# Eleven semaphores fewer in a batched a·bᵀ kernel: stores counted on the loads' semaphores and on five shared ones

## The chip, the cores and the metric

One core of a Trainium2 chip. The metric is the device time of one execution in microseconds (us), as the median of several executions. The record marks each execution as slow when it is over 1.5% above the fastest of its kernel. A ratio and its 95% interval are the record's, from the fast runs of the same rounds, so a ratio is not quite that of the medians quoted beside it. A profile is one execution; its span runs from the first instruction to the last and is about 1.8 us shorter than the measured time.

## The reference

```python
def setup_inputs():
    batch, m, k, n = 16, 512, 512, 512
    return {"a": randn(batch, m, k), "b": randn(batch, n, k)}      # float32

def reference(a, b):
    return np.matmul(a, b.transpose(0, 2, 1)).astype(np.float32)
```

Sixteen products of 512 x 512 matrices: 33.55 MB are read, 16.78 MB written.

## The kernel before

Every engine has its own program; semaphores tie them together. SyncE loads pairs of matrices (16 loads of 2 MB) into seven slots and stores outputs 8 to 15. The first load of b goes out on ScalarE's queue. GpSimd stores outputs 0 to 7 and watches landings to hand the seven output buffers back to ScalarE. VectorE casts to bfloat16, TensorE transposes and multiplies, ScalarE copies the products from PSUM (the memory that TensorE writes to) to the output buffers.

A complete transfer has added 16 to its semaphore: the trace has 16 landings for each, one by one. Each load slot has a semaphore, and so has each of the 16 stores. At the end of the program GpSimd sets all semaphores that the program allocated to zero (`EVENT_SEMAPHORE_RANGE_CLEAR` in the profile, called the clearing below); that instruction is not in the source, the framework adds it.

```python
    STORES = "SSSSOSOSOSSOOOOOO"               # GpSimd: S = store, O = wait for the next landing
    LATE = {11: (8, 9), 13: (10, 11), 15: (12, 13)}
    ...
        s_ld = [sem(f"s_ld{i}") for i in range(NL)]        # NL = 7
        s_st = [sem(f"s_st{i}") for i in range(batch)]     # 16
    ...
        def landed(n):
            return s_st[n], 16

        def store(n):
            engine = nc.gpsimd if n < STORES.count("S") else nc.sync
            engine.wait_ge(s_out, n + 1)
            engine.dma_start(out[n]..., ob[:, n % NO]).then_inc(s_st[n], 16)    # NO = 7

        load(0)
        load(1, nc.scalar)
        for n in range(2, NL):
            load(n)
        for n in range(2 * pairs):
            nc.sync.wait_ge(s_ld[n % NL], 16 * (n // NL + 1)).then_inc(s_go, 1)
            if n > 0 and n + NL - 1 < 2 * pairs:
                load(n + NL - 1)
            for m in LATE.get(n, ()):
                store(m)
        store(batch - 2)
        store(batch - 1)
        for n in range(batch - NO, batch - 1):
            nc.sync.wait_ge(*landed(n))

        n_st = n_of = 0
        nc.gpsimd.wait_ge(s_ld[0], 32)
        for what in STORES:
            if what == "S":
                store(n_st); n_st += 1
            else:
                nc.gpsimd.wait_ge(*landed(n_of)).then_inc(s_of, 1); n_of += 1
    ...     # ScalarE takes one s_of (an output buffer that is free) per output
```

## Time and profile before

| | before |
|---|---|
| median time | 125.56 us (3 runs, 125.42 to 125.84) |
| span of the profile | 123.7 us |
| bytes moved | 50.33 MB |
| rate in mid-stream | 419 to 430 GB/s |
| last copy of ScalarE, last issue of a store | 113.7 us |
| last landing | 122.3 us |
| from there to the end of the span | 1.4 us |

The compute engines finish 8.6 us before the last landing. The lines themselves, and what they say of the bound, stand in the prediction.

### The profile page before, as it was taken

The page shows a single profiled execution, that of the slowest core. Times are in us where ns is not written, and L with a number is a line of the kernel's source. Part 1 is how long each engine was busy: PE and PEld are TensorE (multiplying, and loading weights), DVE is VectorE, ACT ScalarE, POOL GpSimd, SP SyncE. Part 2 cuts the span into 40 slices and gives each one's busy share as a digit, 9 for nine tenths or more (in the row PEclk, how much of TensorE's full clock was granted, in tenths as well). Part 3 has the DMA queues.
Part 4 walks back from the last instruction along what each step waited for, and adds up shares of the span by engine and source line. Part 5 has one row for each costly group of instructions (what it writes and reads, how often), then busy time and mean ns, then how long its engine had stood idle before and what let it go on. Part 6 is the DMA issues. An engine that isn't in the chain of part 4 may idle for free. (4 is left out here: it accounts for less than half of the span.)

```text
span 123.7 us, 2364 instructions
## 1 busy us (share of the span) xinstructions
PE 90.8 (73%) x768; PEld 55.9 (45%) x768; DVE 68.1 (55%) x96; ACT 68.0 (55%) x130; POOL 5.2 (4%) x14
## 2 busy tenths in 40 slices
PE   0000189999999899989998999999899919995000
PEld 0000177447644754674476347645754528441000
DVE  0000698983895689289918974865957078400000
ACT  4000065478855956795589369765946069655000
POOL 2000000000000250001010110000000000000000
PEclk9999999999999999999999999999999986999955
DMA  4999999999999999999999999999999999999990
GB/s 148 413 435 429 429 429 424 429 424 435 435 424 424 429 392 363 445 416 424 453 405 437 443 408 443 424 424 458 397 445 427 408 429 427 429 427 429 424 387 8
DMA packets 4608, 50.33 MB, mean 407 GB/s; under 512 B 512, under 2 KB 512, under 8 KB 512
## 3 DMA queue, kind: packets, MB, share of 16 engines
q1 hardware_dynamic: 3312, 39.85, 76.2%
q0 software_dynamic: 1152, 8.39, 16.1%
q10 hardware_dynamic: 144, 2.10, 4.2%
HBM read 33.55 MB, written 16.78 MB: 407 GB/s over the span
## 5 line engine op out<-in xcount | busy, mean ns | idle before, releaser
L249 PE MATMUL ps<-tb,ta 128*128 128x512 bf16 x256 | 57.8, 379 | 0.5
L207 ACT COPY ob<-ps 128x512 f32 x64 | 34.4, 589 | 29.2 <-PE ps L249 21.3
L189 ACT COPY ta<-tp 128x512 bf16<-128x512 bf16 x64 | 32.9, 610 | 15.0 <-PE tp L230 15.0
L249 PEld LDWEIGHTS ps<-tb,ta 128*128 128x128 bf16 x256 | 24.1, 98 | 30.6 <-issue 4.0
L230 PE MATMUL tp<-ident,ha 128*128 128x128 bf16 x256 | 19.3, 228 | 18.1 <-PEq L135 18.1
L230 PEld LDWEIGHTS tp<-ident,ha 128*128 128x128 bf16 x256 | 16.3, 102 | 21.9 <-issue 20.1
L170 DVE COPY tb<-tp 128x1024 bf16<-128x1024 bf16 x32 | 21.2, 684 | 4.2 <-DVEq L135 4.2
L230 PE MATMUL tp<-ident,hb 128*128 128x128 bf16 x256 | 18.5, 230 | 3.4 <-PEq L135 3.4
L230 PEld LDWEIGHTS tp<-ident,hb 128*128 128x128 bf16 x256 | 16.3, 103 | 4.0 <-issue 4.0
L154 DVE CAST ha<-ld 128x1024 bf16 x8 | 5.5, 687 | 14.3 <-DVEq L135 14.3
L165 DVE COPY ha<-wa 128x2048 bf16<-128x2048 bf16 x8 | 5.5, 691 | 12.7 <-DVEq L135 12.7
L160 DVE CAST wa<-ld 128x2048 bf16 x8 | 9.8, 1220 | 0.0
L160 DVE CAST wb<-ld 128x2048 bf16 x8 | 9.7, 1217 | 0.0
L154 DVE CAST hb<-ld 128x1024 bf16 x8 | 5.5, 692 | 7.3 <-DVEq L135 7.3
L103 POOL DMA_DIRECT2D out_dram<-ob x8 | 4.5, 570 | 65.5 <-DMA ld<-in_b_dram 40.9
L169 DVE COPY hb<-wb 128x2048 bf16<-128x2048 bf16 x8 | 5.5, 685 | 0.1
L157 DVE CAST ha<-ld 128x1024 bf16 x8 | 5.5, 686 | 0.0
L157 DVE CAST hb<-ld 128x1024 bf16 x8 | 5.5, 686 | 0.0
L180 ACT ACT_TABLE_LOAD x1 | 1.3, 1283 | 1.5 <-SPq L43 1.5
L79 POOL TENSOR_SCALAR_AFFINE_SELECT ident<-ident 128x128 bf16<-128x128 bf16 x1 | 0.3, 283 | 0.2 <-POOL ident L77 0.2
L77 POOL MEMSET ident<- 128x128 bf16 x1 | 0.2, 204 | 0.5 <-SPq L43 0.5
L180 ACT COPY one<-const-float32-1.0 128x1 f32<-128x1 f32 x1 | 0.2, 192 | 0.0
(4 smaller groups left out, 0.4 us busy)
## 6 DMA issues: line engine op xcount, KB each, us to landing
ld<-in_a_dram SPq DMA_DIRECT2D x8, 2048.0 KB, 26.5
ld<-in_b_dram SPq DMA_DIRECT2D x7, 2048.0 KB, 29.6
out_dram<-ob POOLq DMA_DIRECT2D x8, 1024.0 KB, 28.9
out_dram<-ob SPq DMA_DIRECT2D x8, 1024.0 KB, 19.7
ld<-in_b_dram ACTq DMA_DIRECT2D x1, 2048.0 KB, 12.0
```

Source lines behind the costliest of these rows:

```text
L103: engine.dma_start(out[n].rearrange("(p j) n -> p j n", j=J), ob[:, n % NO]).then_inc(s_st[n], 16)
L154: nc.vector.tensor_copy(out=h[:, :J, :], in_=src[:, :J, :HK]).then_inc(s_cd, 1)
L157: nc.vector.tensor_copy(out=h[:, J:, :], in_=src[:, J:, :HK]).then_inc(s_c, 1)
L160: nc.vector.tensor_copy(out=w[:], in_=src[:, :, HK:]).then_inc(s_w, 1)
L165: nc.vector.tensor_copy(out=ha[:], in_=wa[:]).then_inc(s_ca, 1)
L169: nc.vector.tensor_copy(out=hb[:], in_=wb[:]).then_inc(s_cb, 1)
L170: nc.vector.tensor_copy(out=tb[:, ko, :], in_=tp[:, 2 + ko % 2].rearrange("k j p -> k (j p)"),).then_inc(s_eb, 1)
L180: nc.scalar.copy(out=one[:], in_=nc.const_aps.tensor(1.0, (P, 1), f32))
L189: c = nc.scalar.copy(out=ta[:, ko, e * J * P:(e + 1) * J * P].rearrange("k (j p h) -> k j p h", j=J, h=2), in_=tp[:, ko % 2, :, e * HP:(e ...
L207: c = nc.scalar.copy(out=dst[:, j, :].rearrange("m (p j) -> m p j", j=2 * J), in_=ps[:, j, :].rearrange("m (j p) -> m p j", j=2 * J),)
L230: t = nc.tensor.transpose(tp[:, 2 * x + g, j, :], h[:, j, g * P:(g + 1) * P], ident[:])
L249: t = nc.tensor.matmul(ps[:, j, :], ta[:, ko, (e * J + j) * P:(e * J + j + 1) * P], tb[:, ko, :].rearrange("k (j p) -> k j p", j=2 * J)[:, ...
```

## The change

The intent is to need fewer semaphores: 34 in place of 45 (of those that the program clears at its end). GpSimd's eight stores take turns on five. SyncE's eight stores count on the semaphores of load slots, with a threshold that counts the loads before them. The description of the change also named the first load of b on ScalarE's queue, but the kernel before already has it there.

```diff
+    SW = 5
-        s_st = [sem(f"s_st{i}") for i in range(batch)]
+        s_st = [sem(f"s_st{i}") for i in range(SW)]
         def landed(n):
-            return s_st[n], 16
+            if n < STORES.count("S"):
+                return s_st[n % SW], 16 * (n // SW + 1)
+            slot = (n - STORES.count("S") + 2) % NL
+            return s_ld[slot], 16 * (len(range(slot, 2 * pairs, NL)) + 1 + (n - STORES.count("S") >= NL))
         ...
-            ).then_inc(s_st[n], 16)
+            ).then_inc(landed(n)[0], 16)
```

## The prediction

> **What bounds the kernel now.** I read four views, in this order: the page's table of 40 slices, its part on DMA queues with the table of stretches, the waits of the DMA-issuing queues, and the one source line that holds the end of the program.
>
> The slices first, because they say which resource is full and when:
>
> ```profile
> PE   0000189999999899989998999999899919995000
> DVE  0000698983895689289918974865957078400000
> ACT  4000065478855956795589369765946069655000
> DMA  4999999999999999999999999999999999999990
> ```
>
> Only the DMA row is at 9 from the second slice to the last but one. TensorE, VectorE and ScalarE start four slices late and have dips; they follow the loads. The bytes and the rate:
>
> ```profile
> HBM read 33.55 MB, written 16.78 MB: 407 GB/s over the span
> ```
>
> 33.55 + 16.78 = 50.33 MB have to move, whatever the semaphores are. The table of stretches (start:end, length, busy time of five engines, granted clock, DMA share, GB/s) shows that the rate is flat:
>
> ```profile
> 10.00:30.00 20.00, 14.09 (x123) 9.62 (x124) 13.47 (x19) 8.97 (x18) 0.00 (x0) 1.00 1.01 430
> 60.00:90.00 30.00, 28.31 (x262) 17.75 (x261) 21.29 (x31) 22.16 (x45) 1.68 (x3) 1.00 1.01 428
> 114.00:118.00 4.00, 0.00 (x0) 0.00 (x0) 0.00 (x0) 0.00 (x0) 0.00 (x0) 1.00 1.01 428
> 120.00:121.00 1.00, 0.00 (x0) 0.00 (x0) 0.00 (x0) 0.00 (x0) 0.00 (x0) 0.50 0.30 123
> ```
>
> 50.33 MB at 428 GB/s are 117.6 us. The span is 123.7 us; the other 6.1 us lie at the two ends: about 1.5 us before data flow and a ramp after it (the first 4 us moved 197 GB/s, which is 4.0 x (1 - 197/428) = 2.2 us lost), and from about 120.3 us on the tail, 3.4 us. The compute is over by 114 us: the last 4 us of full-rate transfers run with no engine busy. The kernel is a full-rate stream of transfers with a start and an end that nothing covers. The chain of waits on the page accounts for only 9% PE and 1% ACT, because it ends at the last ScalarE copy before the last store; the transfers behind that store aren't in it, so here it isn't the view to go by.
>
> The end, from the waits of SyncE's queue (waited for, us in total, times, longest) and from the line that closes the program (durations in ns min/median/max, then start in us):
>
> ```profile
> SPq L121 <- DMA out_dram<-ob: 5.7, 3, 2.4
> SPq L289 <- DMA out_dram<-ob: 1.7, 1, 1.7
> L289 SPq EVENT_SEMAPHORE  x5: 17/28/1680, 120.5 to 123.6; - x5
> L289 POOLq DRAIN  x3: 34/129/714, 120.1 to 123.4; - x3
> L289 POOLq EVENT_SEMAPHORE_RANGE_CLEAR  x1: 287/287/287, 123.1 to 123.1; - x1
> ```
>
> SyncE waits 1.7 us for the last store (the 1680 ns instruction), which lands at about 122.3 us. Then follow a barrier, one instruction of GpSimd that sets the program's semaphores to zero (287 ns at 123.1 us), and another barrier. This last part, 1.4 us, is the only place of the profile where the number of semaphores can show.
>
> **What the Trainium skill says.** "DMA: Bandwidth & Descriptors", section "Why a DMA increments its semaphore by 16 and not by 1", says that each of the 16 transfer engines adds 1 after its own data, and that two transfers in flight on one semaphore can satisfy a wait too early. So sharing is only safe if the first has been waited for before the second is issued; otherwise it costs a race or an added wait. The trace shows the order that the sharing needs, below. The same page, "Anatomy of one DMA — SWDGE (gpsimd) path", gives about 100 ns for the semaphore update after the receipt of the last write, and calls the write of the semaphore on trn2 nearly free: the cost is per transfer, not per semaphore. The number of transfers doesn't change (32 in all). The kernel before agrees in what can be seen: 4-byte packets take 9 ns against 309 ns for an 8192-byte one in the records of the transfers. Its table under "Specifications" names 435 GB/s as the ceiling of the fabric; the steady 428 GB/s here are 98% of it, and the 358 GB/s that it gives as HBM's limit for one core are exceeded, so there the measurement decides. "Runtime: NRT & Kernel Launch", section "The ~15µs preamble/postamble breakdown", has a reset of semaphores outside the kernel with 51 per engine[...]; nothing in this trace shows it.
>
> **The change part by part.** The diff touches no transfer, no queue, no buffer and no compute instruction. The words of the title about the first load of b on ScalarE's queue describe something already in the kernel before: its row of issues has one load of b from ACTq. I compared the order of instructions of both: every engine has the same instructions in the same order, 307 in both programs, and the same places where waits stand. Moved lines are line numbers only.
>
> Stores 0 to 7 (GpSimd) share five semaphores: 0 with 5, 1 with 6, 2 with 7. Store 5 is issued after GpSimd has already waited for store 0, store 6 after store 1, store 7 after store 2; in the kernel before these waits end at 55.4, 62.7 and 70.0 us and the stores are issued at 63.2, 70.5 and 71.1 us. Stores 8 to 15 (SyncE) use the semaphores of load slots 2 to 6, 0, 1 and 2, with a threshold that counts the loads before them. Each of these slots' last load has been waited for by SyncE before the store is issued: the earliest, store 8 at 73.4 us, uses that of load 9, waited for at 58.1 us. Store 15 reuses that of store 8, long landed. So every wait is for the same landing as before, by another number. Added waits: 0. Removed waits: 0. Cost in the stream: 0 us.
>
> What is left is the clearing. The program before clears the semaphores numbered 99 to 143, 45 of them, in 287 ns; if all of that is per semaphore, 6.4 ns each. The changed one clears 99 to 132, 34 of them: estimate 34 x 6.4 = 217 ns, 70 ns less. It stands alone on the path at the end, so all 70 ns would count: 125.56 - 0.07 = 125.49 us, or 0.06%. The three runs before spread over 125.84 - 125.42 = 0.42 us, six times that. I say 125.5 us.
>
> **The rivals.** First: sharing makes a wait longer, such as GpSimd's wait for store 8, now on a semaphore that counts two loads too, or SyncE's closing waits, now on six load semaphores. For it speaks that the waits for landings are real: 24.6 us on GpSimd for stores. Against it: all counted transfers ahead of the awaited one have landed tens of us earlier, and the transfers are full anyway, so a store issued 1 us later would still find others queued. It would make 0 to 0.3 us.
>
> Second: fewer semaphores mean a shorter end, by more than the clearing, if the 714 ns drain of GpSimd or the barriers depended on them. Against it: the drain lies beside SyncE's 1.7 us wait, and the barriers use the same semaphores as before. If the whole clearing vanished, 0.3 us; still 0.2%.
>
> Third: the rate changes, by another interleaving of loads and stores. A GpSimd store issued some ns earlier or later could shift which packets queue where; 1% of the stream is 1.2 us. Against it: the issue times follow from the same events, and the stream sat at 419 to 430 GB/s in every stretch between 10 and 110 us. The straggler at the end is the more sensitive piece: one of the 16 engines ended its last packets 1.1 us after the others (landings at 121.1 and 122.3 us in the trace). Which engine is behind by how much can vary by run, perhaps 0.3 us either way.
>
> **Range and chances.** The centre is 125.5. Spread of the runs before (0.42 us), the straggler and another run's start give about +-0.5 us: 125.0 to 126.0. Faster by over 2% would need 2.5 us, more than the whole end after the last landing (1.4 us), and I see no place for it: 1%. Slower by over 2% would need a wait of 2.5 us in a full stream: 2%. Within 2%: 97%.
>
> **What would show it.** Right: the clearing is shorter than 287 ns (about 217 if the cost is per semaphore, the same if it is fixed), stores are issued at the same times within 0.2 us, the rate in the stretch from 60 to 90 us stays at 428 within 1%, SyncE's closing waits keep 5.7 and 1.7 us within 0.5. Wrong: a gap in the DMA row in the middle, a wait of GpSimd or SyncE that has grown by over 1 us, or an end after the last landing far from 1.4 us.

## The result

The changed kernel took 125.38 us (median of 6 runs, 125.16 to 125.59) against 125.52 us for the kernel before in the same rounds (6 runs, 125.26 to 125.84). The ratio is 0.9986, with a 95% interval from 0.9966 to 1.0006: the same time, by the 2% that counts as a change, and by the interval too.

In its profile the changed kernel moves the same bytes at the same total rate, and its row of 40 slices is the same:

```profile
DMA  4999999999999999999999999999999999999990
HBM read 33.55 MB, written 16.78 MB: 407 GB/s over the span
```

The same stretches as in the prediction (columns as there):

```profile
10.00:30.00 20.00, 14.16 (x106) 9.83 (x107) 13.26 (x18) 8.04 (x16) 0.00 (x0) 1.00 1.01 433
60.00:90.00 30.00, 28.46 (x252) 17.30 (x249) 21.50 (x31) 21.98 (x43) 2.21 (x3) 1.00 1.01 429
114.00:118.00 4.00, 0.00 (x0) 0.00 (x0) 0.00 (x0) 0.00 (x0) 0.00 (x0) 0.93 1.01 426
120.00:121.00 1.00, 0.00 (x0) 0.00 (x0) 0.00 (x0) 0.00 (x0) 0.00 (x0) 0.50 0.20 82
```

429 GB/s from 60 to 90 us where it was 428, and again four full microseconds after the last compute. The stream is what it was. Now the closing waits of SyncE's queue, then the line that closes the program (line 295 here is line 289 of the kernel before; durations in ns min/median/max):

```profile
SPq L127 <- DMA out_dram<-ob: 5.8, 3, 2.4
SPq L295 <- DMA out_dram<-ob: 1.7, 1, 1.7
L295 SPq EVENT_SEMAPHORE  x5: 17/27/1698, 120.4 to 123.5; - x5
L295 POOLq DRAIN  x3: 34/113/714, 120.1 to 123.3; - x3
L295 POOLq EVENT_SEMAPHORE_RANGE_CLEAR  x1: 223/223/223, 123.0 to 123.0; - x1
```

The waits stand at 5.8 and 1.7 us (5.7 and 1.7 before). The clearing fell from 287 to 223 ns. One more number moved: of GpSimd's three drains, the one in the middle fell from 129 to 113 ns. It stands just ahead of the clearing, so it is on the path as well. Together 64 + 16 = 80 ns. The raw records agree: from the last landing to the last instruction it is 1.362 us before (122.259 to 123.621) and 1.281 us after (122.217 to 123.498), 81 ns less. The rest of the difference between the two spans, 0.04 us, is the last landing itself, and that is scatter.

### The profile page after: what moved, and what is told of

Its sections match the earlier page's. It is cut to its first block, busy times and chain, and to the rows that moved or that the text cites. A ratio compares the mean times of both kernels' runs of the same rounds, so it can differ in the third digit from the quotient of the medians.

```text
span 123.5 us, 2364 instructions
## 1 busy us (share of the span) xinstructions
PE 90.7 (73%) x768; PEld 55.8 (45%) x768; DVE 67.9 (55%) x96; ACT 68.1 (55%) x130; POOL 5.9 (5%) x14
## 5 line engine op out<-in xcount | busy, mean ns | idle before, releaser
L236 PEld LDWEIGHTS tp<-ident,ha 128*128 128x128 bf16 x256 | 16.6, 103 | 23.1 <-issue 21.3
L160 DVE CAST ha<-ld 128x1024 bf16 x8 | 5.5, 686 | 13.7 <-DVEq L141 13.7
L109 POOL DMA_DIRECT2D out_dram<-ob x8 | 5.2, 655 | 65.2 <-DMA ld<-in_b_dram 41.1
```

Of the source, the lines that this page charges most:

```text
L109: engine.dma_start(out[n].rearrange("(p j) n -> p j n", j=J), ob[:, n % NO]).then_inc(landed(n)[0], 16)
L160: nc.vector.tensor_copy(out=h[:, :J, :], in_=src[:, :J, :HK]).then_inc(s_cd, 1)
L236: t = nc.tensor.transpose(tp[:, 2 * x + g, j, :], h[:, j, g * P:(g + 1) * P], ident[:])
```

## The experiments

All ten gave a correct result. Seven ran on the chip that the record numbers 2; the run with four stores on one count, the one with GpSimd's stores on SyncE's queue and the last one ran on chip 10, where the kernel before took 125.71 us and not 125.51 to 125.53. Each ratio is within one chip. Two questions were open: is it the count of semaphores that shortens the end, and is the sharing free because the order of events makes it free? The first five runs ask the first, the next three the second, and two go after the other things that the prediction or the description named.

### 100 semaphores more that nothing uses

```diff
 (kernel before)
         s_out = sem("s_out")
+        idle = [sem(f"s_idle{i}") for i in range(100)]
```

> The kernel before with 100 semaphores more that nothing uses, so the program clears 145 instead of 45. Theory (the clearing costs per semaphore: 287 ns for 45 and 223 ns for 34 give 64/11 = 5.8 ns each and about 25 ns fixed): the clearing takes 287 + 582 = about 870 ns, nothing else changes, and the time grows by 0.58 us to about 126.1 (ratio 1.0046 to the kernel before). Rival (the 64 ns were scatter or depend on something else than the count): the clearing stays at 223 to 290 ns and the ratio is 1.000 within its interval. Second rival (more semaphores also slow waits or updates in the stream): the growth is well over 0.6 us and shows before the last landing.

Measured: 126.19 us (126.05 to 126.52, 6 runs) against 125.53 us, ratio 1.0052 (1.0039 to 1.0066). From its closing line:

```profile
L290 POOLq DRAIN  x3: 34/275/714, 120.5 to 124.4; - x3
L290 POOLq EVENT_SEMAPHORE_RANGE_CLEAR  x1: 828/828/828, 123.6 to 123.6; - x1
```

The clearing takes 828 ns (870 expected), 541 more than with 45: 5.4 ns per semaphore. The drain ahead of it takes 275 ns, 146 more than the 129 of before; this was not expected. 541 + 146 = 687 ns, and in the records the stretch from the last landing to the end grew from 1.362 to 2.049 us, the same 687 ns. The time grew by 126.19 - 125.53 = 0.66 us. So the count costs, about 6.9 ns per semaphore between 45 and 145, all of it after the last landing. The first rival falls. The second falls too: from 60 to 90 us the stream ran at 429 GB/s with 145 semaphores.

The time outside the span is 126.52 - 124.7 = 1.8 us in the profiled run, as before (125.48 - 123.7 = 1.8). So nothing outside the span grew with the number allocated. Whether the reset of semaphores outside the kernel that the prediction cited lies in that time, no run here shows.

### The sharing with the count put back

```diff
 (changed kernel)
         s_out = sem("s_out")
+        idle = [sem(f"s_idle{i}") for i in range(11)]
```

> The changed kernel with 11 unused semaphores added, so the sharing stays and the count is 45 as before. Theory (count alone matters): clearing 287 ns again, time equal to the kernel before, ratio 0.9995 to 1.0005 in truth, within an interval of some 0.002. Rival (the sharing itself gains or costs something in the stream): clearing 287 ns but the ratio stays near the 0.9986 of the changed kernel or below, or goes above 1.002.

Measured: 125.52 us (5 runs) against 125.53, ratio 1.0002 (0.9989 to 1.0015).

```profile
L296 POOLq DRAIN  x3: 34/129/714, 120.1 to 123.4; - x3
L296 POOLq EVENT_SEMAPHORE_RANGE_CLEAR  x1: 287/287/287, 123.1 to 123.1; - x1
```

With 45 semaphores both numbers are back to the nanosecond, sharing or not. The sharing by itself does nothing to the time that these runs could see.

### SyncE's part alone, GpSimd's part alone

```diff
 (changed kernel; SyncE's part alone: every store of GpSimd has its own)
-    SW = 5
+    SW = 8
```

> SyncE's part of the change alone: its eight stores use the loads' semaphores, GpSimd's eight keep their own; 37 semaphores cleared. Theory: clearing 287 - 8 x 5.8 = 240 ns, stores issued at the same times within 1 us, ratio 0.9997 in truth, not to be told from 1. Rival (a wait on a load's semaphore ends later): SyncE's closing waits or GpSimd's for store 8 grow by over 1 us.

```diff
 (changed kernel; GpSimd's part alone)
+        s_sp = [sem(f"s_sp{i}") for i in range(8)]
-            slot = (n - STORES.count("S") + 2) % NL
-            return s_ld[slot], 16 * (...)
+            return s_sp[n - STORES.count("S")], 16
```

> GpSimd's part alone: its eight stores share five semaphores, SyncE's keep eight of their own; 42 semaphores cleared. Theory: clearing 287 - 3 x 5.8 = 270 ns, GpSimd's waits for stores unchanged, ratio 0.9999 in truth, not to be told from 1. Rival (sharing delays store 5, 6 or 7): these are issued over 1 us later than 63.0, 70.4 and 70.9 us.

Measured: 125.55 us, ratio 1.0000 (0.9985 to 1.0015), and 125.42 us, ratio 0.9993 (0.9974 to 1.0011). As foreseen, no time tells them apart. The clearing does:

| semaphores | 34 | 35 | 36 | 37 | 42 | 45 | 145 |
|---|---|---|---|---|---|---|---|
| kernel | changed | three on one count | two on one count | SyncE alone | GpSimd alone | before | 100 idle |
| clearing, ns | 223 | 225 | 226 | 243 | 266 | 287 | 828 |
| drain ahead of it, ns | 113 | 119 | 111 | 117 | 124 | 129 | 275 |

(The runs with 35 and 36 come further down.) A straight line through the clearing has 5.4 ns per semaphore and about 40 ns fixed, and the seven values lie within 9 ns of it. The drain rises by 1.5 ns per semaphore from 45 to 145, but from 34 to 45 it isn't even in order: it takes 111 ns with 36. SyncE's closing waits (4.7 us in total for the first group, 1.7 for the last, with SyncE's part alone) didn't come late. With GpSimd's part alone stores 5 to 7 were issued 0.8 to 0.9 us later than the times in the expectation, under the 1 us of the rival, and its first store was already 0.4 us later than in the changed kernel. Neither part holds the whole effect on the clearing; each contributes by its number of semaphores.

### The changed kernel once more

> The changed kernel once more, against the kernel before in five rounds. Theory, sized by the runs so far: the clearing falls by 64 ns and GpSimd's drain ahead of it by 16 ns (129 to 113), together 80 ns or 0.06%, so the ratio is 0.9994 in truth and measured between 0.998 and 1.001. Rival (the 0.9986 of the first comparison was a real gain of 0.17 us in the stream): ratio 0.9986 or below, with an interval that leaves 0.9994 out.

Measured: 125.44 us (125.16 to 125.56, 6 runs) against 125.51, ratio 0.9990 (0.9977 to 1.0003); clearing 223 ns, drain 113 ns. The interval holds both 0.9994 and 0.9986, so this run didn't separate the theory from its rival. What speaks for 80 ns and no more is the sharing with 11 idle semaphores (ratio 1.0002) and the records of the end. A further 0.1 us in the stream is neither shown nor excluded by these times.

### Sharing that lengthens a wait

Three versions of the changed kernel in which the first four, three or two stores count on one semaphore, and each of their waits asks for all of them (34, 35 and 36 semaphores). That is the simple way to share, without the care for order that the change takes.

```diff
 (changed kernel; G = 4, 3, 2 with SW = 5, 6, 7)
-                return s_st[n % SW], 16 * (n // SW + 1)
+                if n < G:
+                    return s_st[0], 16 * G
+                return s_st[n - G + 1], 16
```

> A sharing that does lengthen a wait: stores 0 to 3 count on one semaphore and each of their waits asks for all four (64), with the same 34 semaphores as the changed kernel. The release of the first output buffer moves from 55.2 us to the landing of store 3, about 77 us; ScalarE needs that buffer for output 7 at about 61 us. Theory (the wait has about 6 us of slack and then holds up everything behind it): a stall of ScalarE of about 15 us, of which the backlog of transfers at the end hides a part; time 130 to 140 us. Rival (the transfers are full, so a later wait is hidden): within 1 us of the kernel before. In both the clearing is 223 ns.

Measured with four: 134.43 us (134.32 to 135.12, 4 runs) against 125.71, ratio 1.0707 (1.0672 to 1.0742). Here is ScalarE in order of time (start, us, what, count, idle time before and its cause), first in the changed kernel:

```profile
60.38 1.09 ACT L213 COPY ob<-ps 128x512 f32 x2 [0.59 <-PE ps L255]
62.16 1.07 ACT L213 COPY ob<-ps 128x512 f32 x2 [0.69 <-PE ps L255]
```

and then with the four stores on one count:

```profile
60.08 1.09 ACT L215 COPY ob<-ps 128x512 f32 x2 [0.59 <-PE ps L257]
77.78 2.05 ACT L215 COPY ob<-ps 128x512 f32 x4 [16.61 <-ACTq L143]
```

The copy at 62.16 us is output 7, which needs the buffer of store 0. With all four landings asked for, ScalarE's queue holds it back by 16.6 us until store 3 has landed at 77.5 us. The stream stays full for a long time after (432 GB/s from 60 to 80 us), and then runs dry at the end. The rival, that a full stream hides a later wait, falls for a wait of this length.

> Stores 0 to 2 count on one semaphore and their waits ask for all three (48). The release comes at about 70.1 us, 8 us after ScalarE wants the buffer. Theory (with all four, a delay of 15.6 us at this copy became 13.7 us at the last store and 9.1 us in the span: some 2 us won back, 4.5 us hidden behind the transfers that are still queued): 8.1 - 2 - 4.5 = 1.6 us, time about 127.3. Rival (the backlog hides a share rather than a fixed time, 9.1/15.6 of the delay counts): 4.7 us, time about 130.3.

Measured with three: 127.45 us (126.64 to 128.28, 4 runs) against 125.51, ratio 1.0166 (1.0121 to 1.0211): 1.9 us more, where the fixed-slack theory said 1.6 and the rival 4.7. It is slower than the kernel before, but whether by 2% is unclear, and its four times lie 1.6 us apart; the profiled one took 127.02.

> Stores 0 and 1 count on one semaphore and their waits ask for both (32). The first buffer is released at about 62.7 us instead of 55.2, and ScalarE copies into it at 62.2 us in the changed kernel. Theory (up to 62.2 us the release is free, then 2 us are won back and 4.5 us more are hidden by the backlog of transfers at the end): ScalarE waits about 1 us more, the time is within 0.3 us of the kernel before. Rival (any longer wait counts in full): 0.6 to 1 us longer.

Measured with two: 125.40 us (125.18 to 125.50, 4 runs), ratio 0.9985 (0.9969 to 1.0000). ScalarE did wait 1.6 us for the buffer, and nothing of it arrived in the time.

What of the delay reaches the end can be read from the issues of SyncE's eight stores (start of the first, us from there to the end of the last). In the changed kernel, then with three, then with four:

```profile
74.29 39.55 SPq L109 DMA_DIRECT2D out_dram<-ob  x8
```

```profile
82.99 37.04 SPq L111 DMA_DIRECT2D out_dram<-ob  x8
```

```profile
90.44 37.05 SPq L111 DMA_DIRECT2D out_dram<-ob  x8
```

The last store is issued by 113.84, 120.03 and 127.49 us. With three it is 6.2 us late and the span 1.7 us longer (125.2 against 123.5); with four it is 13.7 us late and the span 9.2 us longer (132.7). Both leave out 4.5 us. This is the slack of that profile: in the changed kernel the last store lands 8.7 us after its issue (113.5 to 122.2 us), behind others; with four, when it finds nothing ahead of it, in 4.2 us (127.2 to 131.3), and 8.7 - 4.2 = 4.5. The slack isn't the same in every run of one kernel. In the second run of the changed kernel the issues were these:

```profile
73.93 42.43 SPq L109 DMA_DIRECT2D out_dram<-ob  x8
```

Here the last store was issued at 116.0 us, 2.5 us later than in the first run, and landed at 122.3, at no cost (125.44 us): 2.0 us of slack were left. What the runs share is the latest moment that costs nothing, 122.2 - 4.2 = 118.0 us for the last issue, an estimate from these landings. With three it was issued at 119.7, with four at 127.2, that is 1.7 and 9.2 us after it, and these are the 1.7 and 9.2 us by which the spans are longer. The rows of the transfers show the hole, with three and then with four:

```profile
DMA  4999999999999999999999999999999999999294
```

```profile
DMA  4999999999999999999999999999999993590094
```

### GpSimd's stores on SyncE's queue

The end shows one of the 16 transfer engines behind the others by 1.1 us. The prediction named it as the sensitive piece of the end. Does it come from the transfers that GpSimd issues?

```diff
 (kernel before)
-    STORES = "SSSSOSOSOSSOOOOOO"
+    STORES = "OOOOOOOOO"
-    LATE = {11: (8, 9), 13: (10, 11), 15: (12, 13)}
+    LATE = {7: (0, 1, 2, 3), 9: (4, 5), 10: (6, 7), 11: (8, 9), 13: (10, 11), 15: (12, 13)}
-        nc.gpsimd.wait_ge(s_ld[0], 32)
```

> The kernel before with GpSimd's eight stores issued from SyncE's queue instead, at about the same times. It asks where the straggler at the end comes from (the last of the 16 engines lands 1.1 us after the others). Theory A (the straggling engine is held up by transfers that GpSimd issues): the last landing is within 0.3 us of the one before it, and the time falls by about 0.8 us, to 124.7. Theory B (it is slower whatever issues the transfers, or the queue order matters more): the straggler stays at about 1 us and the time is the same or up to 2 us worse, as loads and stores now stand in one queue.

Measured: 131.92 us (131.70 to 132.85, 5 runs) against 125.71, ratio 1.0486 (1.0468 to 1.0503). Both theories missed. The last landing is indeed level with the others, within 0.02 us, but only because the stream had run dry before it, as with four stores on one count. In mid-stream the last engine still lands up to 2.3 us behind the median of the 16, with no transfer of GpSimd in the program. There it isn't one engine alone: of the store that landed at 113.52 us, four of the 16 came 0.7 to 2.3 us behind the median, whereas in the kernel before a single one is 1.1 us behind all others. So theory A falls as the sole cause of a lag; the single straggler of the end isn't explained. Theory B was right in kind and far too small in size: 6.2 us, not up to 2. ScalarE again:

```profile
60.25 1.09 ACT L206 COPY ob<-ps 128x512 f32 x2 [0.59 <-PE ps L248]
76.23 2.05 ACT L206 COPY ob<-ps 128x512 f32 x4 [14.88 <-ACTq L134]
```

Store 0 was issued at 49.72 us and landed at 75.93, 26 us later, after five loads issued before it on the same queue; GpSimd's was issued at 42.56 and landed at 55.33, 13 us later, before two loads that SyncE had issued at 34.7 and 37.0 us (landed at 62.5 and 69.8). So it wasn't issued at about the same time, as the expectation had it: of the 20.6 us by which it landed later, 7.2 are the later issue and 13.4 the longer way. Both together brought the same late buffer as the coarse counting, and the same arithmetic holds, against the first profile of the changed kernel: the last store was issued at 125.2 us, 11.7 us late; less 4.5 that makes 7.2, and the span is 130.8 - 123.5 = 7.3 us longer.

### The first load of b on SyncE's queue

```diff
 (changed kernel)
-        load(1, nc.scalar)
+        load(1)
```

> The changed kernel with the first load of b back on SyncE's queue. The title names it on ScalarE's queue, where both kernels have it. Theory: SyncE's issues take about 0.45 us each and the second load comes 0.45 us later, while the first load alone (2 MB, 4.9 us) keeps the transfers full; so the stream starts at the same 1.94 us and the time is the same within 0.3 us. Rival (two queues at the start fill the 16 engines better): the first 4 us move less than 188 GB/s, and the time grows by 0.4 us or more.

Measured: 125.68 us (125.46 to 125.73, 4 runs) against 125.71, ratio 0.9991 (0.9974 to 1.0007). The stretches at the start, first of the changed kernel and then of this one:

```profile
0.00:4.00 4.00, 0.00 (x0) 0.00 (x0) 0.00 (x0) 1.47 (x2) 0.69 (x6) 1.00 0.55 188
4.00:10.00 6.00, 0.00 (x0) 0.00 (x0) 0.00 (x0) 0.00 (x0) 0.00 (x0) 1.00 1.02 434
```

```profile
0.00:4.00 4.00, 0.00 (x0) 0.00 (x0) 0.00 (x0) 1.47 (x2) 0.69 (x6) 1.00 0.55 135
4.00:10.00 6.00, 0.00 (x0) 0.00 (x0) 0.88 (x2) 0.00 (x0) 0.00 (x0) 1.00 1.00 429
```

The first half of the rival came true, 135 GB/s in the first 4 us, and its second half didn't: the busy share of the transfer engines is the same 0.55, and no time was lost. VectorE has its first two casts before 10 us, because the first load now comes alone and lands early; the compute starts sooner and the end doesn't move. So no effect of this piece of the description on the time is seen, wherever the load stands.

## Why the prediction was right

**The bound.** It said that a full-rate stream with uncovered ends sets the time. The result agrees (429 GB/s from 60 to 90 us), and the runs with the coarse counts show how far: the engines cost nothing as long as the last store is issued by about 118 us, which left 4.5 us in the first profile of the changed kernel and 2.0 in the second. One sum was loose: of the 6.1 us put at the two ends, 2.2 + 3.4 = 5.6 lie there. The other 0.5 are in mid-stream, where the rate is a little under 428 (419 GB/s from 30 to 60 us).

**The diff adds and removes no wait.** The code shows it: the order of the instructions is the same in both. The runs agree: with the count put back, the sharing alone gives 1.0002 (0.9989 to 1.0015).

**The clearing.** The estimate was 34 x 6.4 = 217 ns, 70 ns less; measured are 223 ns and 64 less. The estimate laid all 287 ns on the semaphores; about 40 of them are fixed.

**What it left out.** It took the drains for independent of the count, and looked only at the 714 ns one, which does lie beside SyncE's wait. The 129 ns in the very same line of the profile was the drain on the path, and it fell by 16 ns. The sum is 80 ns for the 70 foretold. The two errors, 6 ns too much and 16 ns too little, are far below the scatter of 0.4 us. So the time, 125.38 for the 125.5 foretold, can't tell 70 ns from 80 or from none; the durations at the end and the run with 100 idle semaphores are what bears the mechanism out.

**Rival one, a longer wait.** It didn't happen. Its size was put at 0 to 0.3 us with the argument that a store issued 1 us later finds others queued. For 1 us the run with two stores on one count bears this out (1.6 us of waiting, no cost). For a longer wait the argument is wrong: with four, 16.6 us of waiting cost 8.7 us, because the output buffer behind it holds up all later compute. The 2.5 us of waiting that it gave as enough for a loss of 2% are far from enough: with three, 9.7 us of waiting cost 1.9.

**Rival three, other interleaving.** The rate kept within 1%. The check "issued at the same times within 0.2 us" was too strict: SyncE's first store moved from 73.36 to 74.29 us. With 100 idle semaphores and no sharing it stood at 74.31, and in the sharing kernel with 11 idle ones at 73.39, so this is scatter and not the change. The check on SyncE's closing waits, 5.7 us within 0.5, was met by luck: in seven other runs of the same time within 0.6% the first group was 3.4 to 5.0 us.

**The 358 GB/s.** The prediction called the figure exceeded. "DMA: Bandwidth & Descriptors", section "Measured (HBM→SBUF, 128 partitions, SWDGE, issued from GpSimd)", says of its measurements that they are of a core whose neighbour is idle, and gives 425 GB/s for a load of 16 MB; the 428 here, of loads and stores together, are near that. What the neighbour did here isn't recorded. No step rested on it.

**Open.** Why the drain ahead of the clearing is longer with more semaphores isn't known. Where nothing but the count differs (11 or 100 idle ones) it went from 113 to 129 and from 129 to 275 ns. But it isn't the count alone: with GpSimd's stores on SyncE's queue and 45 semaphores it took 116 ns, not 129, and the order from 34 to 37 is broken (113, 119, 111, 117). In that same run, the only one without transfers of GpSimd, its first drain took 41 ns and not 714. Which engine lags at the end, and why, was not settled either.

## What to carry to other kernels

No cost of a semaphore was seen while a full stream of transfers ran (429 GB/s with 145 as with 34); it cost 5 to 7 ns at the end, where the program clears what it allocated. Sharing was free here, where every wait still stands for the same landing, which needs the earlier transfer to be waited for before the next one on it is issued; a shared count that asks for later landings holds buffers back, and that cost up to 8.7 us. Before calling a longer wait hidden, work out the slack at the end: the time from the last issue to its landing, less what that transfer takes alone. Do so in more than one profile: it was 4.5 and 2.0 us in two runs of one kernel.

## What the Trainium skill lacked or had wrong

- No page has the clearing of a program's own semaphores at its end. "Runtime: NRT & Kernel Launch" has resets outside the kernel only. Here it took 223 ns for 34, 287 ns for 45 and 828 ns for 145 semaphores, about 5.4 ns each and 40 fixed, and the drain ahead of it took 113, 129 and 275 ns.
- "DMA: Bandwidth & Descriptors", section "Rules for kernel authors", says that spreading transfers over the issuing engines does not help bandwidth and only saves sequencer issue time. The rule leaves out that a second queue can bring a store past loads already queued, though the page's section "Queues, rings and completion order" gives the ground for it: a transfer engine takes turns between the queues that have work for it. With the stores on SyncE's queue the first landed 26 us after its issue instead of 13; it was also issued 7.2 us later, and the kernel took 6.2 us longer.
- The same page, section "Latency and other measured facts", has engines 7 and 15 as usually slower and gives as its best guess, marked uncertain, a cause that only GpSimd's transfers have. The profile doesn't name the engines, so whether it is these isn't known; but the last engine was up to 2.3 us behind the median, and three more were behind too, with no transfer of GpSimd in the program.
